# Four due times for q in a hybrid attention kernel: table, statistics, rope and split stand further behind their projection

## The chip, the cores and the metric

The kernel runs on one core of a Trainium2 chip. The core has five engines with a queue each: TensorE (PE in the profile, with PEld for its weight loads), VectorE (DVE), ScalarE (ACT), GpSimd (POOL) and SyncE (SP), which here issues the DMAs. The metric is the device time of one execution in microseconds, lower is better.

## The reference, cut to what matters

A model of four layers over 1040 tokens of width 1024 (16 meta tokens ahead of 1024): sliding-window attention, mLSTM, HGRN2, and sliding-window attention again. Each layer normalises its input, projects it, mixes along the tokens, gates, projects out and adds to the residual. The change concerns the attention layers alone (layers 0 and 3):

```python
q, k, v, z = _split(u @ w_in, (A_W, A_KVW, A_KVW, A_W))
q = rope(rmsnorm(q.reshape(bsz, lp, A_HEADS, A_HD), q_gain), pos)
k = rope(rmsnorm(k.reshape(bsz, lp, A_KV, A_HD), k_gain), pos)
o = sliding_window_attention(q, k, v, sinks, valid)
return (o * jax.nn.silu(z)) @ w_out
```

There are 16 query heads and 4 key heads of 64, so q fills eight tiles of 128 rows and k two.

## The kernel before

Activations lie transposed: features on the 128 partitions, tokens along the row, in three chunks of 400, 384 and 256 tokens (in layer 3 the first chunk of q has 384). Every product in full precision is three products of halves: an operand is cast to its high part (`uh`, `wh`, `yh`, `qs`, on ScalarE, L194, L463) and the rest is subtracted (`ul`, `wl`, on VectorE, L195, L464). A projection of one tile over one chunk (`proj`, L228) is four quarters of six matmuls, which gather in one PSUM bank. There are eight banks, shared with the mixers.

The order of TensorE's work is written by hand: a list of steps, each a counted cost in nanoseconds (from 1/2.4 ns a column; 960 for a quarter of a 384-wide chunk), a function that issues instructions, and for some a load ahead. TensorE follows this list exactly. For the other engines the list gives ranks: a planner puts their instructions in order by its own reckoning of when each is ready, and among ready ones takes the one that stands first in the list; the mixers' steps are moved 40 instructions ahead in rank. So the place of a step without matmuls is a rank, not a time.

For one piece of q (tile t, chunk n) the work after its projection is:

- eviction (`evac`): the scaled copy `dst` and the square `sq` (ScalarE, L492, L493), then four DMAs that copy `dst` with its halves exchanged to `rot` (L496, on SP's queue). The three lie in temporaries, tag `t`, of which there are six (`TMPS`), shared with the normalising steps, v's eviction and the gates.
- `factors`: the chunk's rope table `cs` is loaded (L503) if another chunk's is there; it has one buffer.
- `stat_q`: small matmuls sum the squares of each head (L516), ScalarE makes the inverse root (L518, L519). Here `sq` comes free.
- `rope`: three VectorE products and sums (L530 to L532). Here `rot` comes free.
- `q_split`: two casts (L463) and two subtractions (L464) into four buffers a chunk. Here `dst` comes free. A score product (S step, L621) reads the result.

Where each of the four stands is given by `D_Q`, counted from the end of the piece's projection:

```python
return [(D_Q[0], [0.0, factors, None]), (D_Q[1], [108 * len(CHUNK_BLOCKS[n]), stat_q, None]),
        (D_Q[2], [0.0, rope, None]), (D_Q[3], turn)]
```

k has the same chain with `D_K`, with whole-tile statistics (L525) and its first tile in rows instead of temporaries. `chain` adds up the projections of a stage and sorts these due times; `spread` puts each step ahead of the first quarter whose start, in counted time of projections, is not before it; what is due after the stage hangs over into the next one. A split that would stand ahead of the S step that frees its buffers is set back to that S step (L748 to L754).

The normalising steps of the next chunk (`Norm.unit`, L386 and the split L194, L195) are put into the finished list by `later`, eight for a chunk, at due times of their own; a step passes behind steps of no cost that stand at its place. The first layer's head does k's first tile and q's first two by chunks; layer 3's head does k and q's first tile by chunks and then q's second tile. After the head, `weave` merges the mixers (S: scores and softmax; T: transposes, L647, two units behind; V: the product with v, L666, four units behind) with projections, in proportion to counted cost.

Of the kernel before, what the change touches and what calls it, by code (L numbers as in the profile page):

```python
# [46 lines left out]
PARTS = 4  # L47
FIRST = (0.2, 0.8, 0.85), (0.2, 0.75, 0.8)
D_K = 2000.0, 4000.0, 6000.0
D_Q = 1500.0, 2500.0, 3500.0, 4500.0  # L50


MM = 1.0 / 2.4
# [58 lines left out]
def hybrid_kernel(ctx: ExitStack, tc: tile.TileContext, ins, out, layers=(0, 1, 2, 3)):  # L112
# [303 lines left out]
    def layer_a(i, j, first, last, fin):  # L416
# [69 lines left out]
        def qk_proj(src, gcol, work, fsplit, ch, t=None):  # L486
# [11 lines left out]
            def finish(n, c0, cn):  # L498
# [38 lines left out]
                if t is not None:  # L537
                    return [(D_Q[0], [0.0, factors, None]), (D_Q[1], [108 * len(CHUNK_BLOCKS[n]), stat_q, None]),
                            (D_Q[2], [0.0, rope, None]), (D_Q[3], turn)]
                return [(D_K[0], [4 * cn * MM, stat, None]), (D_K[1], [0.0, rope, None]), (D_K[2], turn)]  # L540
# [963 lines left out]
```

## Time and profile before

| | |
|---|---|
| median of 3 runs | 2632.33 us (2629.12 to 2633.46) |
| the profiled execution's own time | 2634.16 us |
| its span, first to last instruction | 2632.4 us |
| TensorE busy | 2570.6 us (98%) |
| VectorE busy | 1976.7 us (75%) |
| ScalarE busy | 1667.5 us (63%) |
| GpSimd busy | 249.6 us (9%) |
| mean granted TensorE clock | 0.992 |

How to read it: a timeline row is start, length, engine, source line, operation, what it writes and from what, the shapes, how often; in brackets the idle time of the engine before it and what ended that. A row of waits is the waiting engine with its instruction, what it waited for, and us in total, times, longest. In a table of stretches each engine's busy time stands in the order PE, PEld, DVE, ACT, POOL, followed by the granted clock as a share of full speed, the DMA share and GB/s. Layer 0 runs from the start to about 500 us, layer 3 from about 2180 us to the end.

### The profile page before, as it was taken

What the parts mean: (1) busy time and instruction counts of PE and PEld (TensorE: products, weight loads), DVE (VectorE), ACT (ScalarE), POOL (GpSimd) and SP (SyncE); (2) the same over time, 40 slices, a digit from 0 to 9 for tenths busy, and PEclk for the clock granted to TensorE, in tenths of its full rate; (3) what the DMA queues carried; (4) which work ended last, traced back from release to release, by engine and by line L of the source; (5) the groups of instructions that cost most, each with busy time, mean ns of one, the idle gap of its engine ahead of it and who ended that gap; (6) DMA issues with size and microseconds to landing.
All of it is one profiled execution on the core that took longest, in us unless ns stands there. A gap on an engine that the chain in (4) does not pass through costs nothing.

```text
span 2632.4 us, 54257 instructions
## 1 busy us (share of the span) xinstructions
PE 2570.6 (98%) x20422; PEld 2488.0 (95%) x20422; DVE 1976.7 (75%) x5296; ACT 1667.5 (63%) x4374; POOL 249.6 (9%) x502
## 2 busy tenths in 40 slices
PE   7999999989999999999999999999999999999999
PEld 5999989989999999999999999999999998999999
DVE  6797788784747474747475688989887978887996
ACT  6676767565454545454545757878685857767772
POOL 2221231000000000000000000100000000321330
PEclk9999999999999999999999999999999999999999
DMA  4212111011111111111111101111110113212112
GB/s 130 67 50 84 54 44 47 21 63 52 41 57 41 57 41 57 41 53 45 53 45 49 53 30 42 34 35 34 35 41 30 38 50 90 58 46 84 55 38 80
DMA packets 82583, 135.92 MB, mean 52 GB/s; under 512 B 12033, under 2 KB 35713, under 8 KB 82321
## 3 DMA queue, kind: packets, MB, share of 16 engines
q1 hardware_dynamic: 82320, 132.45, 15.7%
q8 instruction: 161, 2.64, 0.4%
q14 instruction: 102, 0.83, 0.1%
HBM read 117.56 MB, written 4.26 MB: 46 GB/s over the span
## 4 chain that ended last, share of the span: by engine, by line
PE 76%; DVE 12%; ACT 7%; issue 2%; DMA 2%; POOL 1%; SPq 0%; DVEq 0%; ACTq 0%; POOLq 0%
PE pj L228 36%; PE pj L322 16%; PE pj L277 10%; PE po L666 2%; PE pt L647 1%; ACT Sm L632 1%; PE po L910 1%; PE pa L924 1%; DVE wl L195 1%; PE po L912 1%; DVE Sm L629 1%; PE pj L273 1%; DVE qs L464 1%; DVE Pl L650 1%; PE pm L1162 1%
## 5 line engine op out<-in xcount | busy, mean ns | idle before, releaser
L228 PE MATMUL pj<-uh,wh 128*128 128x256 f32 (+2 forms) x2688 | 917.8, 341 | 8.4 <-ACT uh L194 8.4
L228 PE MATMUL pj<-ul,wh 128*128 128x256 f32 (+2 forms) x2688 | 868.8, 323 | 3.7 <-DVE ul L195 3.5
L228 PE MATMUL pj<-uh,wl 128*128 128x256 f32 (+2 forms) x2688 | 866.4, 322 | 0.0
L228 PEld LDWEIGHTS pj<-uh,wh 128*128 128x128 f32 x2688 | 511.4, 190 | 25.3 <-ACT uh L194 11.6
L228 PEld LDWEIGHTS pj<-ul,wh 128*128 128x128 f32 x2688 | 511.6, 190 | 12.5 <-DVE ul L195 7.4
L228 PEld LDWEIGHTS pj<-uh,wl 128*128 128x128 f32 x2688 | 510.8, 190 | 0.0
L194 ACT CAST wh<-wr 128x512 fp32r<-128x512 f32 (+1 forms) x338 | 203.3, 613 | 110.2 <-PE pj L322 31.2
L195 DVE TENSOR_TENSOR wl<-wr,wh 128x512 fp32r<-128x512 f32 (+1 forms) x338 | 233.9, 701 | 51.9 <-ACT wh L194 49.4
L322 PE MATMUL pj<-yh,wh 128*128 128x384 f32 (+2 forms) x768 | 254.2, 331 | 9.0 <-DVE x L325 6.6
L325 DVE TENSOR_TENSOR x<-x,pj 128x384 f32<-128x384 f32 (+2 forms) x480 | 234.9, 508 | 34.5 <-PE pj L322 33.0
L322 PE MATMUL pj<-yl,wh 128*128 128x384 f32 (+2 forms) x768 | 246.3, 321 | 0.0
L322 PE MATMUL pj<-yh,wl 128*128 128x384 f32 (+2 forms) x768 | 246.2, 321 | 0.0
L277 PE MATMUL pj<-wh,uh 128*128 128x256 f32 (+1 forms) x768 | 232.2, 302 | 0.0
L277 PE MATMUL pj<-wl,uh 128*128 128x256 f32 (+1 forms) x768 | 216.8, 282 | 0.0
L277 PE MATMUL pj<-wh,ul 128*128 128x256 f32 (+1 forms) x768 | 216.4, 282 | 0.0
L635 POOL TENSOR_TENSOR Sm<-Sm,s 128x512 f32<-128x512 f32 (+2 forms) x136 | 141.3, 1039 | 459.6 <-DVE s L634 450.2
L632 ACT ACTIVATE Sm<-Sm,s 128x257 f32<-128x257 f32 (+2 forms) x272 | 131.0, 483 | 83.0 <-DVE s L629 79.9
L404 ACT ACTIVATE t<-t 128x384 f32<-128x384 f32 (+2 forms) x240 | 117.9, 491 | 86.8 <-DVE t L403 85.2
L403 DVE SCALAR_TENSOR_TENSOR t<-pj,t 128x384 f32<-128x384 f32 (+2 forms) x192 | 98.9, 515 | 79.5 <-ACT t L402 77.5
L322 PEld LDWEIGHTS pj<-yh,wh 128*128 128x128 f32 x768 | 145.1, 189 | 13.6 <-DVE x L325 8.5
L194 ACT CAST yh<-r 128x384 fp32r<-128x384 f32 (+2 forms) x120 | 57.1, 478 | 149.4 <-PE pj L322 137.3
L277 PEld LDWEIGHTS pj<-wh,uh 128*128 128x128 f32 x768 | 144.7, 188 | 2.1
(255 smaller groups left out, 5438.3 us busy)
## 6 DMA issues: line engine op xcount, KB each, us to landing
wr<-in_b_win SPq DMA_DIRECT2D x124, 256.0 KB, 2.8
wr<-in_a_win SPq DMA_DIRECT2D x80, 256.0 KB, 2.8
wr<-in_c_win SPq DMA_DIRECT2D x64, 256.0 KB, 2.7
wr<-in_a_wout SPq DMA_DIRECT2D x32, 256.0 KB, 2.8
wr<-in_b_wout SPq DMA_DIRECT2D x32, 256.0 KB, 2.7
t<-t SPq DMA_DIRECT2D x104, 48.0 KB, 1.9
cs<-in_rope SPq DMA_DIRECT2D x11, 400.0 KB, 3.3
cs<-in_rope SPq DMA_DIRECT2D x11, 384.0 KB, 3.2
```

The costliest lines, as they stand in the source:

```text
L194: s.copy(h, src)
L195: v.tensor_tensor(l, src, h.bitcast(F32), op=ALU.subtract)
L228: pe.matmul(acc[:, :cn], a[:, k, :], b[:, k, c0 : c0 + cn], start=(k == 0 and i == 0), stop=(k == KT - 1 and i == 2))
L273: pe.matmul(acc[:48, :nc], um[0][:, k, :], m[:, kk, :], start=(k == 0 and m is wh), stop=(k == KT - 1 and m is wl))
L277: pe.matmul(acc[:cn, :nc], a[:, k, c0 : c0 + cn], m[:, kk, :], start=(k == 0 and j == 0), stop=(k == KT - 1 and j == 2))
L322: pe.matmul(acc[:, :cn], a[:, k, mc], b, start=(k == 0 and i == 0), stop=(k == 1 and i == 2))
L325: v.tensor_tensor(x[:, m, c0 : c0 + cn], x[:, m, c0 : c0 + cn], acc[:, :cn], op=ALU.add)
L403: v.scalar_tensor_tensor(a[:, :cn], z, 0.0, a[:, :cn], op0=ALU.min, op1=ALU.subtract)
L404: s.activation(a[:, :cn], a[:, :cn], AF.Exp)
L632: s.activation(Sm[:nq, u, : nk + 1], Sm[:nq, u, : nk + 1], AF.Exp, scale=-1.0, bias=st[:nq, u : u + 1], accum_out=den[:nq, u : u + 1])
L635: g.tensor_tensor(Sm[:nq, :, :nk], Sm[:nq, :, :nk], den[:nq].rearrange("p (u c) -> p u c", c=1).to_broadcast([nq, 2, nk]), op=ALU.mult)
L666: pe.matmul(po[:, :, q0 - g0 : q0 - g0 + nq], V[pair // 2, kb][:kn, P * hh : P * hh + P], w[part][:kn, ki, :, :nq], start=(ki == 0 and par ...
```

## The change

The four due times of q's steps behind the end of their projection become later: the table's request, the statistics and the rope by 500 ns of counted time, the split by 1500. Nothing else changes: the same instructions on the same engines.

```diff
 D_K = 2000.0, 4000.0, 6000.0
-D_Q = 1500.0, 2500.0, 3500.0, 4500.0
+D_Q = 2000.0, 3000.0, 4000.0, 6000.0
```

## The prediction

> **What bounds the kernel.** I read the page first, then TensorE's waits in the two attention layers, then the timeline where they lie, then the clock in small stretches.
>
> ```profile
> span 2632.4 us, 54257 instructions
> PE 2570.6 (98%) x20422; PEld 2488.0 (95%) x20422; DVE 1976.7 (75%) x5296; ACT 1667.5 (63%) x4374; POOL 249.6 (9%) x502
> ...
> PE pj L228 <- ACT uh L194: 7.1, 6, 2.7
> ...
> PE pj L228 <- ACT uh L194: 1.3, 2, 0.8
> ...
> PE pa L516 <- ACT t L493: 0.2, 1, 0.2
> ```
>
> TensorE is busy in 98% of the span, so only its idle time and its slow time can change. The change touches layers 0 and 3 alone. The third row is from TensorE's waits in 0 to 528 us, the last two from those after 2100 us (us in total, times, longest). TensorE hardly waits for q's own statistics (0.2 us), so nothing is won there directly. It waits for normalised input (uh) at the heads of the layers, and, as part (4) shows, for the softmax before the first transposes. These two are what q's rope and split stand beside.
>
> ```profile
> 64.00:74.20 10.20, 9.27 (x40) 8.24 (x39) 6.90 (x15) 4.32 (x12) 0.00 (x0) 0.50 0.21 60
> 2207.60:2214.30 6.70, 6.70 (x31) 6.48 (x32) 5.65 (x11) 3.03 (x8) 0.00 (x0) 0.50 0.38 108
> ...
> 60.60:64.00 3.40, 1.84 (x8) 1.24 (x9) 3.21 (x9) 3.32 (x9) 0.00 (x0) 1.00 0.00 0
> 2204.10:2207.50 3.40, 1.94 (x8) 1.02 (x7) 2.96 (x8) 2.77 (x8) 0.00 (x0) 1.00 0.14 51
> 40.10:43.50 3.40, 2.19 (x14) 1.61 (x13) 3.40 (x8) 2.13 (x6) 0.00 (x0) 1.00 0.25 63
> 255.10:258.50 3.40, 2.46 (x14) 2.07 (x13) 1.74 (x3) 3.37 (x8) 0.00 (x0) 1.00 0.70 195
> 2323.60:2327.00 3.40, 2.07 (x12) 1.55 (x11) 2.92 (x6) 3.22 (x9) 1.63 (x2) 1.00 0.06 21
> ...
> 2202.42 0.28 PE L228 MATMUL pj<-ul,wh 128*128 128x256 f32 x1
> 2202.54 0.28 PE L228 MATMUL pj<-uh,wl 128*128 128x256 f32 x1
> 2210.42 0.42 PE L228 MATMUL pj<-uh,wh 128*128 128x256 f32 x1
> 2210.63 0.42 PE L228 MATMUL pj<-ul,wh 128*128 128x256 f32 x1
> ```
>
> The first column after the stretch is its length, then TensorE's busy time; the 0.50 or 1.00 is the granted clock. The waits at the heads are followed by stretches at half clock: 10.2 us in layer 0, 6.7 us in layer 3. A 256-column matmul then starts every 0.21 us instead of 0.12, so a half-clock stretch costs 0.45 of its length: 4.6 and 3.0 us. The 3.4 us before a drop (rows three to five, all followed by half clock) hold 1.84 to 2.19 us of busy TensorE; rows six and seven, with 2.46 and 2.07, were not followed by one. I take about 2.2 us as the border.
>
> **The change, part by part.** No instruction is added or removed. For each of the 48 pieces of q (8 tiles, 3 chunks, 2 layers) four steps move: the rope table's request by 500 ns, the statistics by 500, the rope by 500, the split by 1500, in the code's own counted nanoseconds. A quarter projection counts 960 for a 384-wide chunk, so most steps slip one or two quarters.
>
> (1) Head of layer 3. From the start of the head k's and q's first chunk count 7840; q's statistics are due at 7840+2500=10340, its rope at 11340. Quarters of k's second chunk end at 8800, 9760, 10720, 11680. So before, the rope stands ahead of the second chunk's first q quarter, and with it ahead of the last (eighth) normalising step of chunk 2, which goes behind it. After, 10840 and 11840 put both behind that step. What that order costs now:
>
> ```profile
> 2204.71 0.39 PE L228 MATMUL pj<-uh,wh 128*128 128x256 f32 x1 [0.51 <-ACT uh L194]
> 2203.85 0.48 DVE L386 SCALAR_TENSOR_TENSOR t<-x,ngain,v 128x256 f32<-128x256 f32 x1
> 2205.03 0.55 DVE L530 TENSOR_TENSOR t<-t,cs 128x384 f32<-128x384 f32 x1
> 2206.01 0.55 DVE L531 TENSOR_TENSOR t<-t,cs 128x384 f32<-128x384 f32 x1
> 2206.48 0.48 DVE L386 SCALAR_TENSOR_TENSOR t<-x,ngain,v 128x256 f32<-128x256 f32 x1
> 2206.99 0.40 ACT L194 CAST uh<-t 128x256 fp32r<-128x256 f32 x1 [0.49 <-DVE t L386]
> 2207.45 0.53 PE L228 MATMUL pj<-uh,wh 128*128 128x256 f32 x1 [0.79 <-ACT uh L194]
> ```
>
> Two rope products (2 x 0.5 us) run between the seventh and the eighth normalising product (L386); the eighth's cast ends as the matmul starts that had waited 0.79 us. With the rope behind it the eighth comes up to 1.0 us sooner: -0.8 us. The 3.4 us before the drop would then hold 1.94+0.79=2.7 us, above the border, and the drop goes: -3.0 us. Late next is the sixth step's cast behind k's split, which the change leaves (a wait of 0.5 us at 2204.71).
>
> The Trainium skill, "TensorE: Matmul & The Clock Gate", Part 1, says the clock halves after at least one idle window of about 3.4 us. The lengths 10.2 and 6.7 us agree with its window; that the drop needs an idle window does not, since 1.94 us were busy. By that rule term (1) would be -0.8 instead of -3.8.
>
> (2) Head of layer 0, chunk 2. There q's second chunk ends at a count of 19680; its statistics go from 22180 to 22680 and its rope from 23180 to 23680. The other q tile's quarters begin at 19680, 20640, 21600 and 22560, k's third chunk at 23520. So the statistics move from ahead of the seventh normalising step to behind the eighth, and the rope from ahead of the eighth to behind it.
>
> ```profile
> 58.32 0.27 ACT L518 ACTIVATE rq<-pa,eps 128x6 f32<-128x6 f32 x1 [0.73 <-PE pa L516]
> 61.07 0.38 PE L228 MATMUL pj<-uh,wh 128*128 128x256 f32 x1 [0.93 <-ACT uh L194]
> 63.97 0.48 DVE L386 SCALAR_TENSOR_TENSOR t<-x,ngain,r 128x256 f32<-128x256 f32 x1
> 64.36 0.55 DVE L530 TENSOR_TENSOR t<-t,cs 128x384 f32<-128x384 f32 x1
> ...
> 66.10 0.48 DVE L386 SCALAR_TENSOR_TENSOR t<-x,ngain,r 128x256 f32<-128x256 f32 x1
> 67.09 0.58 PE L228 MATMUL pj<-uh,wh 128*128 128x256 f32 x1 [0.52 <-ACT uh L194]
> ```
>
> ScalarE stood 0.73 us for q's statistics (L518) with casts of the input behind it, and TensorE then waited 0.93: between 0 and -0.9, I take -0.5, as k's split stays ahead of the later casts. Rope products again run ahead of the last normalising product: between 0 and -0.5, I take -0.4, because six temporaries (t) are shared with q and the slot may come no sooner. The 3.4 us before the drop would hold 1.84+0.5=2.3, just over the border. I count one of the three windows, 3.4 x 0.45 = -1.5 (ends 0 and -4.6).
>
> (3) First chunk boundary of layer 0. There q's and k's ropes only change places ahead of the eighth step; a product more or less of 0.5 us: -0.5 to +1.0, taken as 0.
>
> (4) First mixer units. Which quarter of v's projection falls between the first S step and its T step follows from the weaving of the two lists by counted time, and one statistics step now falls behind the head.
>
> ```profile
> 87.23 0.27 PE L647 MATMUL pt<-ident,Sm 16*16 16x16 f32 x2 [1.52 <-POOL Sm L635]
> 2239.01 0.66 PE L647 MATMUL pt<-ident,Sm 128*128 128x128 f32 x4 [2.62 <-POOL Sm L635]
> ...
> 2188.35 0.34 PE L228 MATMUL pj<-uh,wh 128*128 128x384 f32 x1
> 2188.53 0.34 PE L228 MATMUL pj<-ul,wh 128*128 128x384 f32 x1
> ```
>
> Counted, layer 0 has 2400 ns between them and gets 1440; layer 3 has 1440 and gets 2400. The difference is one quarter, six 384-column matmuls at 0.175 us, 1.05 us. So the wait of 1.52 becomes about 2.6, the wait of 2.62 about 1.6: +1.05 and -1.05, together 0 (each may miss by its 1.05).
>
> (5) The other 40 or so pieces, beside the mixers.
>
> ```profile
> ACT qs L463 <- DVE t L532: 11.1, 16, 1.7
> ...
> 116.79 0.57 DVE L532 TENSOR_TENSOR t<-t,t 128x400 f32<-128x400 f32 x1
> 118.24 1.08 ACT L463 CAST qs<-t 64x400 fp32r<-64x400 f32 x2
> ...
> 336.75 0.28 PE L228 MATMUL pj<-uh,wl 128*128 128x256 f32 x1
> 339.40 0.45 ACT L492 ACTIVATE t<-pj,cons 128x256 f32<-128x256 f32 x1
> 360.04 0.18 PE L621 MATMUL pm<-r,qs 128*16 128x16 f32 x1 [1.98 <-DVE Pl L650]
> 360.90:364.30 3.40, 3.40 (x15) 2.91 (x14) 2.07 (x8) 1.45 (x7) 0.41 (x2) 0.50 0.00 0
> ```
>
> The split's cast follows the rope within a microsecond or so, and ScalarE even stood for the rope 16 times: the planner runs these steps when their data are there, and their place in the list is a rank among ready work. Later rank costs nothing while the first S that reads the piece is far. By the counted order the nearest is in layer 3, where ten steps remain of sixteen. So 0, between -1 and the price of the slots in the rivals. TensorE's statistics products (L516) move with unchanged number and wait for less than 0.2 us: 0. On SP's queue the rope table's load moves as far as the rope that reads it, so its lead of 2000 stays; q's rotated copies (L496) are issued at the eviction and don't move, and neither they nor weights queue longer behind it: 0. POOL has none of these steps.
>
> Sum: -0.8 -3.0 -0.5 -0.4 -1.5 +1.05 -1.05 = -6.2 us. The profiled execution took 2634.16 us, so 2628.0 by its own time; it lay 1.8 us above the median of the runs, 2632.33, and from that the sum gives 2626.1 us. A change within 0.2% (5.3 us) can't be told from none.
>
> **Rivals.** *The place hardly matters, or the clock falls anyway.* If the eighth step was held by its temporary's slot rather than by rank, term (1) and (2) stay undone; for it speaks that the six temporaries serve both; against it that at this place in layer 3 only one piece of q holds any, k's products being in rows. If the clock falls all the same, -0.8 -0.9 = -1.7 are left: 2630.6. The skill's rule on the idle window, cited above, leads to this case too.
>
> *Slower: late evictions.* Each piece of q holds three of six temporaries: the square until the statistics, the rotated copy until the rope, the scaled copy until the split. All are now held longer. Going through the new order, seven would be wanted at once at 7 places in layer 0 instead of 4, at 8 in layer 3 instead of 4. One such place is shown above: the last piece of q was evicted 2.4 us after its last matmul (336.75 + 0.28 to 339.40), and 20 us later TensorE stood 1.98 us and lost 3.4 x 0.45 = 1.5 us to the clock (the two last rows above). That is 3.5 us a place, if the one caused the other, which the trace doesn't show. From two places on it outweighs the gain; with four of the seven new ones, +14 -1.7 and the first T of layer 0 at its worst, +1: 2646; with three, 2641.
>
> *Faster still.* All of 10.2 us at half clock goes: 3.1 us more, 2623; with the full 0.9 and 0.5 of term (2) 2622.
>
> **How the numbers follow.** The forecast with its faster variant 0.42, no effect or clock anyway 0.27, late evictions 0.31. These are also the chances of faster, same and slower. The time is the forecast's, 2626.1. The likeliest case alone spans 2620 to 2629. The range takes the faster end with the doubtful terms (3) and (4) at their good ends, 2618, and three to four late places, 2645.
>
> **What would show it.** In the after profile, if right: the normalising products L386 of chunk 2 in layer 3 run without L530 and L531 between the last two, the wait of 0.79 us at about 2207 and the half clock behind it are gone; in layer 0 the half clock at 64 us is shorter; the first transpose waits about 2.6 us in layer 0 and 1.6 in layer 3. Wrong if the rope still runs between the last two L386, if the clock drops without that wait, or if evictions L492 lag their projection by over 2 us at more places and new waits of TensorE beside the mixers follow.

## The result and the profile after

| | before | after |
|---|---|---|
| median | 2630.87 us (18 runs, 2626.03 to 2633.66) | 2626.08 us (18 runs, 2623.87 to 2629.02) |
| ratio, 95% interval | | 0.9983 [0.9976, 0.999] |
| profiled execution, own time and span | 2634.16, 2632.4 us | 2624.74, 2623.0 us |

The change is worth 4.8 us by the medians, 0.18%. The interval lies clear of 1, though the gain is a little under the 0.2% taken as the bound. The two profiled executions differ by 9.4 us, almost twice as much, and the first task is to see why.

The page of the kernel after, its first lines:

```profile
span 2623.0 us, 54248 instructions
PE 2565.2 (98%) x20422; PEld 2484.6 (95%) x20422; DVE 1970.6 (75%) x5296; ACT 1665.7 (64%) x4374; POOL 249.8 (10%) x502
```

TensorE still bounds the kernel. To place the difference, I take the same projection matmul (the n-th of the 10368 at L228 and L277) in both traces and compare when it starts:

| place | before, us | after, us | after ahead by |
|---|---|---|---|
| behind layer 0's head and first mixer units | 100.23 | 100.81 | -0.58 |
| within layer 0's mixers | 260.09 | 259.53 | 0.56 |
| near their end | 379.90 | 377.21 | 2.69 |
| end of layer 0 | 495.95 | 493.21 | 2.74 |
| layer 3's head, where k's split ends | 2203.01 | 2198.99 | 4.02 |
| end of layer 3's head | 2216.16 | 2208.22 | 7.94 |
| first S steps of layer 3 | 2232.27 | 2224.67 | 7.60 |
| behind the first T and V steps | 2245.06 | 2241.39 | 3.68 |
| end of layer 3's mixers | 2523.14 | 2513.77 | 9.37 |

Four stretches at half clock of the profile before have no counterpart after (stretches of the kernel before; the fourth, at 360.9 us, was shown in the prediction):

```profile
87.90:91.30 3.40, 3.40 (x16) 2.85 (x14) 2.11 (x9) 2.07 (x11) 0.24 (x2) 0.50 0.32 113
1654.60:1658.00 3.40, 3.40 (x14) 3.38 (x13) 3.35 (x13) 1.92 (x7) 0.00 (x0) 0.50 0.00 0
2504.50:2507.90 3.40, 3.40 (x16) 3.40 (x15) 2.10 (x8) 0.46 (x2) 0.00 (x0) 0.50 0.00 0
```

The one at 87.9 us lies ahead of the table's first place and is counted there. The other three cost 3 x 3.4 x 0.45 = 4.6 us, and 9.4 - 4.6 = 4.8, the difference of the medians. They can't be put down to the change. Two kernels of the experiments keep layer 0's old due times (layer 3 alone, one piece), and neither has the one at 361 us. The one at 1655 us lies in layers 1 and 2, which are the same in 12 of the kernels here; 4 of the 12 profiles show it. The last section takes the one at 2504 us. So I leave the three out of the account of the change. That the rest then meets the medians so well is luck in part, since the half clock in the heads varies between executions too (experiment 1).

Now the prediction's main place, layer 3's head, in the timeline of the kernel after (start, length, engine, line, operation):

```profile
2199.74 0.48 DVE L386 SCALAR_TENSOR_TENSOR t<-x,ngain,v 128x256 f32<-128x256 f32 x1
2200.69 0.39 PE L228 MATMUL pj<-uh,wh 128*128 128x256 f32 x1 [0.51 <-ACT uh L194]
2201.01 0.48 DVE L386 SCALAR_TENSOR_TENSOR t<-x,ngain,v 128x256 f32<-128x256 f32 x1
2201.99 0.55 DVE L530 TENSOR_TENSOR t<-t,cs 128x384 f32<-128x384 f32 x1
2202.79 0.55 DVE L531 TENSOR_TENSOR t<-t,cs 128x384 f32<-128x384 f32 x1
```

Both rope products now stand behind the last L386. Of the two waits of 0.51 and 0.79 us only the first is left, and the 6.7 us at half clock are gone.

Some 30 us later the gain is lost again. Timeline of the kernel after: TensorE's waits at the first V step, VectorE's order ahead of them, and ScalarE's cast.

```profile
2236.57 0.55 PE L666 MATMUL po<-Ph,v 128*128 128x256 f32 x1 [3.31 <-DVE v L587]
2237.81 0.58 PE L666 MATMUL po<-Ph,v 128*128 128x256 f32 x1 [0.47 <-DVE v L587]
...
2228.92 0.56 DVE L530 TENSOR_TENSOR t<-t,cs 128x384 f32<-128x384 f32 x1 [0.34 <-DMA cs<-in_rope]
2232.14 1.14 DVE L464 TENSOR_TENSOR qs<-t,qs 64x384 fp32r<-64x384 f32 x2
2233.30 0.42 DVE L530 TENSOR_TENSOR t<-t,cs 128x256 f32<-128x256 f32 x1
2234.65 0.65 DVE L532 TENSOR_TENSOR t<-t,t 128x256 f32<-128x256 f32 x1
2236.15 0.28 DVE L587 TENSOR_TENSOR v<-pt,v 16x128 fp32r<-16x128 f32 x1
...
2229.88 0.26 ACT L586 CAST v<-pt 16x128 fp32r<-16x128 f32 x1
```

The cast of v's first block was done at 2230.1. Its subtraction, 0.28 us of work, ran six us later, behind the rope and split of q's second tile. The matmul that needed it had waited 3.31 us. The stretch at half clock that begins within that wait, kernel after:

```profile
2235.30:2242.10 6.80, 5.06 (x22) 4.80 (x23) 3.59 (x12) 3.16 (x10) 1.22 (x2) 0.50 0.20 57
```

By its length it costs up to 6.8 x 0.45 = 3.1 us more; its first 1.3 us still belong to the wait.

Layer 0's head, timeline of the kernel after:

```profile
45.41 0.69 PE L228 MATMUL pj<-uh,wh 128*128 128x384 f32 x1 [2.90 <-ACT uh L194]
63.56 0.38 PE L228 MATMUL pj<-uh,wh 128*128 128x256 f32 x1 [1.42 <-ACT uh L194]
66.33 0.55 DVE L530 TENSOR_TENSOR t<-t,cs 128x384 f32<-128x384 f32 x1
67.14 0.55 DVE L531 TENSOR_TENSOR t<-t,cs 128x384 f32<-128x384 f32 x1
67.61 0.48 DVE L386 SCALAR_TENSOR_TENSOR t<-x,ngain,r 128x256 f32<-128x256 f32 x1
68.90 0.48 DVE L386 SCALAR_TENSOR_TENSOR t<-x,ngain,r 128x256 f32<-128x256 f32 x1
89.28 0.20 PE L647 MATMUL pt<-ident,Sm 16*16 16x16 f32 x2 [1.18 <-POOL Sm L635]
```

Its two stretches at half clock:

```profile
44.00:54.20 10.20, 8.79 (x29) 8.49 (x30) 6.61 (x11) 8.46 (x21) 5.15 (x7) 0.50 0.19 53
64.40:78.10 13.70, 12.03 (x48) 10.41 (x47) 9.58 (x21) 7.25 (x19) 0.00 (x0) 0.50 0.17 45
```

Here the rope still runs ahead of the last two L386, and the half clock got longer, 13.7 us instead of 10.2. At the first chunk boundary (44 us) it is 10.2 instead of 6.8.

### The profile page after: what moved, and what is told of

It is laid out like the page before. It is cut to its first block, busy times and chain, and to the rows that moved or that the text cites. A ratio compares the mean times of both kernels' runs of the same rounds, so it can differ in the third digit from the quotient of the medians.

```text
span 2623.0 us, 54248 instructions
## 1 busy us (share of the span) xinstructions
PE 2565.2 (98%) x20422; PEld 2484.6 (95%) x20422; DVE 1970.6 (75%) x5296; ACT 1665.7 (64%) x4374; POOL 249.8 (10%) x502
## 5 line engine op out<-in xcount | busy, mean ns | idle before, releaser
L228 PE MATMUL pj<-uh,wh 128*128 128x256 f32 (+2 forms) x2688 | 916.4, 341 | 9.6 <-ACT uh L194 9.6
L228 PE MATMUL pj<-ul,wh 128*128 128x256 f32 (+2 forms) x2688 | 867.9, 323 | 2.2 <-DVE ul L195 1.7
L228 PE MATMUL pj<-uh,wl 128*128 128x256 f32 (+2 forms) x2688 | 864.6, 322 | 0.0
L228 PEld LDWEIGHTS pj<-uh,wh 128*128 128x128 f32 x2688 | 510.2, 190 | 26.8 <-ACT uh L194 13.2
L228 PEld LDWEIGHTS pj<-ul,wh 128*128 128x128 f32 x2688 | 510.5, 190 | 11.1 <-DVE ul L195 5.8
L228 PEld LDWEIGHTS pj<-uh,wl 128*128 128x128 f32 x2688 | 510.0, 190 | 0.0
L322 PE MATMUL pj<-yh,wh 128*128 128x384 f32 (+2 forms) x768 | 253.0, 329 | 8.0 <-DVE x L325 6.2
L322 PE MATMUL pj<-yh,wl 128*128 128x384 f32 (+2 forms) x768 | 245.2, 319 | 0.0
L322 PE MATMUL pj<-yl,wh 128*128 128x384 f32 (+2 forms) x768 | 245.2, 319 | 0.0
L277 PE MATMUL pj<-wh,uh 128*128 128x256 f32 (+1 forms) x768 | 231.9, 302 | 0.0
L277 PE MATMUL pj<-wl,uh 128*128 128x256 f32 (+1 forms) x768 | 216.5, 282 | 0.0
L277 PE MATMUL pj<-wh,ul 128*128 128x256 f32 (+1 forms) x768 | 216.2, 281 | 0.0
L322 PEld LDWEIGHTS pj<-yh,wh 128*128 128x128 f32 x768 | 144.2, 188 | 11.7 <-DVE x L325 7.4
L277 PEld LDWEIGHTS pj<-wh,uh 128*128 128x128 f32 x768 | 144.6, 188 | 2.1
```

Source lines behind the costliest of these rows:

```text
L228: pe.matmul(acc[:, :cn], a[:, k, :], b[:, k, c0 : c0 + cn], start=(k == 0 and i == 0), stop=(k == KT - 1 and i == 2))
L277: pe.matmul(acc[:cn, :nc], a[:, k, c0 : c0 + cn], m[:, kk, :], start=(k == 0 and j == 0), stop=(k == KT - 1 and j == 2))
L322: pe.matmul(acc[:, :cn], a[:, k, mc], b, start=(k == 0 and i == 0), stop=(k == 1 and i == 2))
```

## The experiments

In the kernels of experiments 1 to 3 a line is added ahead of the functions and another in them, so L386 reads L387, L530 to L532 read L531 to L533, and L587 reads L589.

**1. One layer at a time.** The new due times in layer 3 alone, and in layer 0 alone.

```diff
+D_Q2 = 2000.0, 3000.0, 4000.0, 6000.0
-                    return [(D_Q[0], [0.0, factors, None]), ...
+                    d = D_Q2 if i == 3 else D_Q        # the second kernel: i == 0
+                    return [(d[0], [0.0, factors, None]), ...
```

> The new due times in layer 3 alone, layer 0 as before. In the two profiles the changed kernel is level with before at the head of layer 3 but for 4.0 us won earlier, then 8.0 ahead behind the head, 4.0 ahead behind the first mixer units, 9.4 at the end. Theory A (the gain is made in layer 3, by the head and by stalls beside the mixers, less the new wait at the first V step): ratio to before 0.998 (-5 us). Theory B (the gain is layer 0's, or scatter of the clock's drops between executions): 1.000. Either way the half clock behind the head of layer 3 is gone, if the rank of q's rope was its cause.

> The new due times in layer 0 alone. Theory A: -0 to -2.7 us, that is 0.999 to 1.000; the head of layer 0 wins nothing (its two half-clock stretches stay), and the 2.7 us seen at its end hang on one drop of the clock at about 361 us. Theory B (layer 0 carries the gain): 0.998.

Layer 3 alone: 2627.64 us, ratio 0.9992 [0.9983, 1.0001]. Layer 0 alone: 2628.12 us, ratio 0.9992 [0.9983, 1.0001]. Before on the same chip took 2630.22 us. Each half alone can't be told from no change; together they multiply to 0.9984, about what the whole gives. Theory A's 0.998 for layer 3 alone and theory B's 0.998 for layer 0 alone both lie outside their intervals, so neither layer carries the whole gain. Layer 0 does its share, although its head hardly improves. Measured by the start of the same matmuls against the profile before, the kernel with layer 0 changed is 0.62 us ahead behind that head, the one with layer 0 unchanged 0.65 us behind: such differences lie within what executions of the same head show. Over the profiles here that place is reached at 99.80 to 100.88 us with layer 0's old due times (three profiles) and at 98.55 to 101.03 us with the new ones (five). Beside the mixers the first wins 3.5 us, the second 1.15. Neither has the drop to half clock at 361 us, 1.5 us, which is about the second's gain; the other 2 us are the change's. This part repeats: from that place to the end of layer 0 the two profiles with the old due times and without the drop take 394.5 and 394.6 us, the five with the new ones 392.0 to 392.5. In layer 3 the head wins 3.9 us, and the wait of 3.3 us at the first V step takes it back. How much that head wins hangs on the clock too: with layer 0 alone changed, the old wait of 0.80 us at layer 3's head is followed by 3.4 us at half clock and not 6.7, and the head takes 11.74 us, against 13.15 in the profile before and 9.23 to 9.27 with the new due times. By this profile it wins 2.5 us.

**2. One piece, and one tile back.** First only the piece whose rope stood in the way (q tile 0, chunk 0 of layer 3). Then the whole change without q tile 1's later chunks in layer 3, the pieces behind which v's subtraction queued.

```diff
+                    d = D_Q2 if i == 3 and t == 0 and n == 0 else D_Q            # one piece
+                    d = D_Q2 if not (i == 3 and t == 1 and n > 0) else D_Q       # one tile back
```

> One single piece moved: q's first tile, first chunk, in layer 3; the other 47 as before. This is term (1) of the prediction alone. Theory A: the wait of 0.8 us at the last normalising step and the half clock behind it go, -3.8 us, ratio 0.9985. Rival (the clock drops anyway, or the drop is made up for later): -0.8 us or nothing, ratio 0.9997 to 1.000. The first transpose of layer 3 still waits about 2.6 us in both.

> The changed kernel, with the second and third chunk of q's second tile in layer 3 put back to the old due times. Theory A (their late rope and split are what holds up v's subtraction, for which the first V step of layer 3 then waits 3.3 us, with a half-clock stretch of 6.8 us behind it): that wait and the half clock go, 6.8 us, and the old wait of 2.6 us at the first transpose comes back: about -4 us against the changed kernel, ratio to before 0.9966. Rival (the V step waits because it stands nearer to its T step in the new order): the wait stays, ratio as the changed kernel's, 0.998.

One piece: 2631.85 us, ratio 1.0006 [0.9998, 1.0015], which is the rival's number. At the end of the head the profiled execution has won the full 3.9 us (1.55 us ahead at its middle, 5.48 at its end), and 16 us later 1.74 are left. One tile back: 2625.85 us, ratio 0.9982 [0.9973, 0.9991], no better than the change. TensorE's timeline after the head, first of the kernel with one piece, then of the one with a tile back:

```profile
2224.29 0.83 PE L517 MATMUL pa<-masks,t 128*128 128x2 f32 x6 [1.63 <-ACT t L494]
```

```profile
2219.22 0.83 PE L517 MATMUL pa<-masks,t 128*128 128x2 f32 x6 [1.14 <-ACT t L494]
2231.72 1.12 PE L649 MATMUL pt<-ident,Sm 128*128 128x128 f32 x4 [2.14 <-POOL Sm L637]
```

With the other pieces' statistics at their old places, TensorE comes to the statistics (L517) before ScalarE has made the square (L494). What the head wins is only kept if the steps behind it move too. In the kernel with a tile back, the wait for v fell to 0.5 us and the transposes' old wait came back (2.14 us), as I had expected. I had not expected the wait for the square nor two stretches of 3.4 us at half clock, and with them nothing was won. One such stretch follows the wait of 1.63 us in the first kernel too.

**3. The split alone, and the rest without the split.**

```diff
+D_Q2 = 1500.0, 2500.0, 3500.0, 6000.0        # split alone
+D_Q2 = 2000.0, 3000.0, 4000.0, 4500.0        # without the split
```

> Only the split of q is due later (6000 instead of 4500); the table, the statistics and the rope keep their old places. Theory (the place of statistics and rope counts): at the head of layer 3 the rope's first products run ahead of the eighth normalising product again, the wait of about 0.8 us and a stretch at half clock are back, and the ratio to the kernel before is 1.000, between 0.9993 and 1.0007. Rival (the gain comes from the later split, which no longer stands ahead of softmax work beside the mixers): the gains at about 2300 to 2350 and 2450 to 2510 us are there without the one at the head, about 5 us, and the ratio is 0.998.

> The table, the statistics and the rope of q are due 500 later as in the change; the split stays at 4500. Theory (the place of statistics and rope counts): the whole gain of 4 us at the head of layer 3 is there, ratio 0.998 to 0.9990; the wait of 3.3 us for v's subtraction at the first V step stays if the later rope causes it, for the rope stands ahead of that subtraction either way. Rival (the later split counts): ratio 1.000, and the wait for v's subtraction is gone, since it would be the split's doing.

Split alone: 2628.22 us, ratio 0.9994 [0.9985, 1.0003]; the wait of 0.80 us at layer 3's head and a 3.4 us stretch at half clock are back, as the theory has it. Without the split: 2629.38 us, ratio 0.9997 [0.9988, 1.0006] (before: 2630.61 us). There the head wins its 3.9 us, but the theory's total fails, because the wait at the first V step grew (timeline of the kernel without the split):

```profile
2240.00 0.55 PE L668 MATMUL po<-Ph,v 128*128 128x256 f32 x1 [4.88 <-DVE s L636]
2239.14 0.42 DVE L465 TENSOR_TENSOR qs<-t,qs 64x256 fp32r<-64x256 f32 x1
2239.58 0.28 DVE L589 TENSOR_TENSOR v<-pt,v 16x128 fp32r<-16x128 f32 x1
```

The wait is put down to `s`, but that row names what came last by the profile; the subtraction of v (L589) runs at 2239.58 to 2239.86, just ahead of the matmul, and behind the last piece's split (L465). So the later split is worth something: it lets v's subtraction pass one step earlier. Neither half gives the change's 0.9983. Beside layer 3's mixers (2245 to 2523 us) the kernel without the split wins 5.4 us, as the change does (5.7), and the split alone nothing (0.1): that gain belongs to the statistics and the rope. The drop at 2504 us, 1.5 us, is part of it in the first two. Beside layer 0's mixers, with the drop at 361 us left out, the kernel without the split wins 0.9 us of the change's 1.8, and the split alone none.

**4. v's subtraction ahead of the rope.** The change, with v's first tile in layer 3 due 500 behind its projection instead of 1500.

```diff
-                return [(D_V, [108 * len(CHUNK_BLOCKS[n]), fn, None])]
+                return [(500.0 if last and jj == 0 else D_V, [108 * len(CHUNK_BLOCKS[n]), fn, None])]
```

> The changed kernel with one more step moved: in layer 3 the first tile of v is evicted and split 500 counted ns behind its projection instead of 1500, so that its subtraction stands ahead of the second q tile's rope and not behind it. Theory (VectorE's order holds that subtraction, and the wait gives back what the head has won): the first V step no longer waits 3.3 us, the half clock of 6.8 us behind the wait goes with it, and the kernel is 3.8 (wait and 0.5) to 6.9 us (with 6.8 x 0.45 of the clock) shorter than the changed one: ratio to the kernel before 0.9957 to 0.9968. Rival (something else is as late there, as it was with the second tile's pieces at their old places): a wait of 1 to 3 us for the softmax or for q's statistics takes its place, and the ratio stays at 0.998.

2621.88 us, ratio 0.9967 [0.9955, 0.998]. This is the theory's range: 4.2 us below the change by the medians. The upper end of the interval still reaches the rival's 0.998, but its five runs (2620.16 to 2622.35 us) lie below all 18 of the change. The timeline on VectorE:

```profile
2227.83 0.28 DVE L587 TENSOR_TENSOR v<-pt,v 16x128 fp32r<-16x128 f32 x1
2228.70 0.56 DVE L530 TENSOR_TENSOR t<-t,cs 128x384 f32<-128x384 f32 x1 [0.59 <-DMA cs<-in_rope]
```

TensorE's waits from 2190 to 2250 us (us in total, times, longest):

```profile
PE pt L647 <- POOL Sm L635: 0.9, 2, 0.6
PE pj L228 <- ACT uh L194: 0.5, 1, 0.5
```

The stretch across the old wait, at full clock:

```profile
2228.00:2242.00 14.00, 13.30 (x98) 12.59 (x97) 12.90 (x37) 9.83 (x33) 4.29 (x8) 1.00 0.28 87
```

0.28 us of work, moved ahead of the rope, takes away 3.8 us of waiting and the half clock behind it. That it was VectorE's order that held v, and nothing else as late, is shown.

**5. What holds the rope ahead in layer 0.** First the change with the rope and split of q's second chunk 2500 later still in layer 0; then the change with seven temporaries instead of six (and two gated outputs instead of three, for the room, which disturbs all that follows, so that only the head is read).

```diff
+ (D_Q[2] + 2500.0 * (i == 0 and n == 1 and t < 2), [0.0, rope, None]), (D_Q[3] + 2500.0 * (...), turn)]
```
```diff
-ROWS, TMPS, RAWS, YS = 8, 6, 2, 3
+ROWS, TMPS, RAWS, YS = 8, 7, 2, 2
```

> The changed kernel with the rope and the split of the first two q tiles' second chunk in layer 0 another 2500 counted ns later, which puts them far behind the eighth normalising step of the third chunk. If their rank is what holds that step back, the eighth normalising product runs ahead of the rope's three products and the stretch at half clock at 64 us gets shorter than 13.7 us. If the temporary it writes to is what holds it (six are shared with q), rank makes no difference: the rope still runs ahead of the last normalising product, and half clock stays between 10 and 14 us there.

> The changed kernel with seven temporaries instead of six, and two buffers instead of three for the gated output to make room (that disturbs the projections out, so only the first 100 us are read). If the slots hold the last normalising steps of the third chunk in layer 0, a seventh lets the last two go with one rope product ahead of them instead of three, and the half clock at 64 us shrinks by one window of 3.4 us or more from 13.7 us. If not, the same order and the same 10 to 14 us.

With the rope later (2625.68 us, one run), the order on VectorE and the clock stay as they are in the change. With seven temporaries, one rope product instead of two stands ahead of the seventh L386, and the eighth follows it at once. Timeline of VectorE, first the kernel with the later rope, then the one with seven temporaries:

```profile
66.54 0.55 DVE L530 TENSOR_TENSOR t<-t,cs 128x384 f32<-128x384 f32 x1
67.35 0.55 DVE L531 TENSOR_TENSOR t<-t,cs 128x384 f32<-128x384 f32 x1
67.81 0.48 DVE L386 SCALAR_TENSOR_TENSOR t<-x,ngain,r 128x256 f32<-128x256 f32 x1
```

```profile
66.27 0.55 DVE L530 TENSOR_TENSOR t<-t,cs 128x384 f32<-128x384 f32 x1
67.07 0.87 DVE L386 SCALAR_TENSOR_TENSOR t<-x,ngain,r 128x256 f32<-128x256 f32 x2
67.86 0.55 DVE L531 TENSOR_TENSOR t<-t,cs 128x384 f32<-128x384 f32 x1
```

Their stretches at half clock, in the same order:

```profile
64.70:78.40 13.70, 12.02 (x47) 10.50 (x47) 9.49 (x21) 7.16 (x19) 0.00 (x0) 0.50 0.17 45
```
```profile
66.60:76.80 10.20, 9.98 (x42) 9.16 (x42) 6.93 (x15) 4.64 (x14) 0.00 (x0) 0.50 0.21 60
```

So in layer 0's head, by one profile of each kernel, the slots and not the later rank set that order: the last normalising products have no temporary to write to, and the planner fills the time with the rope that is ready. The window of half clock that goes (13.7 to 10.2) may be the clock's chance (10.2 was seen with the same order and six, in experiment 4), so its price stays open. That kernel took 2667.43 us as a whole, which I put down to the two gated outputs; it says nothing of the head, and was not taken apart.

**6. Shorter holding in layer 0.** On top of experiment 4, the first two q tiles of layer 0 get earlier due times. First all four, then all but the split.

```diff
+                    d = (500.0, 1000.0, 2000.0, 3000.0) if i == 0 and t < 2 else D_Q      # all four
+                    d = (1000.0, 1500.0, 2500.0, 6000.0) if i == 0 and t < 2 else D_Q     # all but the split
```

> The changed kernel with v's first step early as in the run before, and in layer 0 the four steps of the first two q tiles brought forward to 500, 1000, 2000 and 3000 instead of 2000, 3000, 4000 and 6000, so that each piece holds its three temporaries for a shorter time. Theory (in layer 0's head the normalising steps of the next chunk wait for those temporaries): the eight products of the third chunk come sooner, no rope stands ahead of the last one, the half clock at 64 us shrinks from 10 to 14 us to 7 us or less, and the kernel is 1.5 to 4.5 us shorter than with v's step alone: ratio 0.995 to 0.9962. Rival (the work itself, ropes and splits, fills VectorE there in any order): what is brought forward stands ahead of the first of the eight instead of the last, TensorE waits as long, and the ratio stays at 0.9967.

> As the run above, with the steps of those two tiles at 1000, 1500, 2500 and 6000: the square and the rotated copy come free sooner, the scaled copy as late as in the change. Theory (temporaries): half of the gain of the run above, since two of three slots come free early and k's and q's splits stay behind the normalising steps: ratio 0.9955 to 0.9967. Rival (order alone): the rope ahead of the first normalising steps costs what the later ones win, ratio 0.9967 or above.

All four: 2621.08 us, ratio 0.9966 [0.9954, 0.9978], as without it, which is the rival's number. The half clock behind 65 us did shrink to 6.8 us, as the theory has it, but TensorE waited 4.45 us for ScalarE's square at 67.2 us, where all four came too early. All but the split: 2618.62 us, ratio 0.9952 [0.994, 0.9965], a little below the theory's range and the fastest of all. Its half clock in the head, from 40 us on:

```profile
42.80:46.20 3.40, 3.34 (x11) 2.83 (x10) 3.34 (x6) 2.71 (x8) 2.27 (x3) 0.50 0.19 47
63.30:70.10 6.80, 6.44 (x26) 5.66 (x27) 4.49 (x11) 4.61 (x13) 0.00 (x0) 0.50 0.13 33
```

10.2 us at half clock, against 17.0 in experiment 4 and 23.9 in the change; 3.3 us by the medians against experiment 4. That short holding is the cause is made likely by experiment 5 and not shown apart from the new order itself.

## Why the prediction was right in its time and partly wrong in its steps

The forecast of 2626.1 meets the median of 2626.08, and the direction was the forecast's. That the two agree so closely is luck, twice over. The sum was taken from 2632.33 us, the median of three runs; from the 2630.87 us of the 18 runs, -6.2 would have made 2624.7. And within the sum the errors of the steps cancel. By the table of starts, without the three stretches that come by chance, with a loss as plus:

| step of the prediction | forecast, us | measured, us |
|---|---|---|
| (1) head of layer 3 | -3.8 | -3.9 |
| (2) to (4) in layer 0's head | -1.35 | +0.6 |
| (4) first mixer units of layer 3 | -1.05 | +4.3 |
| (5) beside the mixers, layers 0 and 3 | 0 | -6.0 |
| layers 1 and 2, untouched | 0 | +0.2 |
| sum | -6.2 | -4.8 |

(The measured rows: 7.94 - 4.02; 0.58; 7.94 - 3.68; then 2.74 + 0.58 - 1.5 = 1.8 and 9.37 - 3.68 - 1.5 = 4.2; 4.02 - 2.74 - 1.5.)

**(1) was right** in its mechanism: the rope went behind the eighth step, the wait of 0.79 us and its 6.7 us at half clock left. Its size is that of this pair of profiles; with one window of half clock behind the same wait, as in experiment 1, it is 2.5 us. The border of 2.2 us is not sharp either: 2.07 us in the prediction's own seventh row was not followed by a drop. The Trainium skill's rule ("TensorE: Matmul & The Clock Gate", Part 1), which asks for an idle window ahead of a drop, would have made it -0.8; the measured 3.9 speak against it here. Experiment 2 adds what the prediction lacked: alone, this step gives nothing, because the next late work stands close behind.

**(2) was wrong at its first step.** The head gave no gain that can be told from its scatter (experiment 1). The prediction read from counted times that the rope would fall behind the eighth normalising step. The list said so, but the built order did not follow it. The first rival named the reason for both heads ("held by its temporary's slot rather than by rank"), and I set it aside by an argument that holds for layer 3 alone. Experiment 5 shows that the slot sets the order. The three waits there (0.93, 0.78 and 0.52 us) became 1.42, 0.53 and 0.50, together 0.2 us more. The half clock grew by 3.4 us instead of shrinking by one window: 13.7 us in four of the five profiles with the new layer 0, 10.2 in the fifth and in all three with the old one.

**(3)** was taken as 0 with ends at -0.5 and +1.0. Timeline and stretch of the kernel before, there:

```profile
44.28 0.69 PE L228 MATMUL pj<-uh,wh 128*128 128x384 f32 x1 [1.81 <-ACT uh L194]
46.45 0.69 PE L228 MATMUL pj<-ul,wh 128*128 128x384 f32 x1 [1.49 <-DVE ul L195]
```
```profile
43.50:50.30 6.80, 4.54 (x13) 4.14 (x14) 6.58 (x10) 5.11 (x12) 4.06 (x5) 0.50 0.00 0
```

One wait of 2.90 us took the place of these two, and the half clock went from 6.8 to 10.2 us; two of the five profiles with the new layer 0 have 6.8 us there as before, so the longer stretch is not the change's alone. The step's range did not contain a window of the clock, though (1) had just priced one.

**(4)** was wrong in layer 0: 1.18 us instead of about 2.6. A wait that the prediction did not name went as well, that of the first V step in the kernel before:

```profile
94.39 0.25 PE L666 MATMUL po<-Ph,v 16*128 16x32 f32 x1 [1.40 <-DVE v L587]
```

It is gone too in the kernel without the split and stays, with 1.41 us, in the one with the split alone, so the statistics and the rope decide it. The stretch at 87.9 us came by chance: the kernel with layer 3 alone has the same wait of 1.52 us ahead of it and no half clock behind. From 35 to 100 us TensorE's waits of over 0.4 us add up to 9.0 us before and 7.5 after, the half clock to 20.4 and 23.9 us, which costs 1.5 us more; so this head as a whole stands about where it stood.

In layer 3 the wait for the softmax left altogether, more than the 1.05 forecast, so the quarter between S and T may have come as reckoned. But what is late next was not asked. It was v's subtraction, which had been hidden behind the T step's wait and now stood alone, behind two ropes and a split on VectorE: +4.3 us. The prediction named what queues for q's own chain and not what queues behind q on VectorE. Experiment 4 shows this cause and its price.

**(5)** was taken as 0 down to -1. It gave 6.0 us, in both layers. Layer 0's 1.8 us repeat (experiment 1). Layer 3's 4.2 us are less firm: with the drop at 2504 us left out, that part takes 275.6 to 276.6 us in three profiles with the old due times there (one piece among them) and 272.4 to 273.7 in three with the new ones, so 1.9 to 4.2 us. In layer 3 the statistics and the rope bring it and not the split; in layer 0 they bring half of it alone (experiment 3). In layer 3 part of it can be named. TensorE's waits of 2300 to 2520 us add up to 6.6 us before and 5.0 after; two of the larger rows of before are gone, and a large one of after is new (us in total, times, longest):

```profile
PE pj L322 <- DVE t L411: 0.9, 1, 0.9
PE pj L322 <- DVE Pl L650: 0.7, 2, 0.5
```
```profile
PE pj L322 <- DVE r L675: 1.0, 1, 1.0
```

The sum falls by 1.6 of the 4.2 us. The rest lies in gaps that I have not taken apart, and why a later rope shortens them stays open. The error was to read "TensorE hardly waits for q" as "q's place costs nothing": q's steps stand ahead of other work on VectorE and ScalarE.

**The slower rival**, late evictions, did not happen: evictions (L492) that start over 2 us behind their last matmul number 15 before (8 in layer 0, 7 in layer 3) and 13 after (5 and 8), and the one that the prediction showed starts 2.0 us behind instead of 2.4. (Its 2641 us for three late places leaves out the +1 that its 2646 for four has.) The shortage of temporaries that I counted did bite, but in layer 0's head, on the normalising steps; one eviction there went from 4.0 us behind (at 63.47) to 5.1 (at 65.87).

## What to carry to other kernels

When a step is moved back on a busy in-order engine, ask first whose small operation stands behind it there; 0.28 us of subtraction in the wrong place cost 3.8 us of waiting and a half clock. A later rank in a list moves nothing where a buffer decides, so before counting on a new order, count who holds the buffers at that place. And a gain at one place is kept only if the next late thing is moved with it: find it before summing.

## What the runs showed of the hardware that I had not expected

The same stall may or may not halve the clock, by where it falls in a fixed grid of 3.4 us (the stretches at half clock shown here last one to four times that). In layer 3 the wait for the residual (L322) is the same in the kernel of experiment 4 (2.16 us at 2491.12) and in the change (2.16 us at 2495.56). Stretches on the grid of each: first the kernel of experiment 4, then the change.

```profile
2488.40:2491.80 3.40, 1.24 (x9) 1.00 (x8) 3.33 (x8) 0.92 (x3) 1.09 (x2) 1.00 0.00 0
2491.80:2495.20 3.40, 3.40 (x15) 3.40 (x14) 2.51 (x8) 0.00 (x0) 0.00 (x0) 0.50 0.00 0
```

```profile
2491.30:2494.70 3.40, 2.10 (x15) 1.81 (x13) 3.28 (x11) 2.40 (x8) 1.35 (x3) 1.00 0.00 0
2494.70:2498.10 3.40, 2.54 (x17) 2.54 (x18) 3.39 (x9) 0.00 (x0) 0.00 (x0) 1.00 0.00 0
```

In the first the stall lies within one window, TensorE is busy for 1.24 of 3.4 us, and the next window runs at half clock. In the second the grid cuts it, 2.10 and 2.54 us are left busy, and the clock stays. Twelve of the profiles here have this wait with 2.13 to 2.17 us, 2.13 in the kernel before (at 2503.36); seven are followed by half clock, the kernel before among them, and five are not. The Trainium skill says that the window runs freely of the kernel ("TensorE: Matmul & The Clock Gate", Part 1, under what is actually happening); these rows agree. So a single trace can show 1.5 us per stall that the next execution lacks, and two profiles can differ by 4.6 us more than the kernels do.
